# Keys, values and half of the queries of an attention stage as seven block products in two groups, in a one-core encoder trunk

## The chip, the core and the metric

The kernel runs on one core of a Trainium2 chip. The metric is the device time of one execution in microseconds (us). Engines are called as in the profile: PE is TensorE (matrix products), PEld its weight loads, DVE is VectorE, ACT is ScalarE, POOL is GpSimd, SP is SyncE, which issues most DMAs.

## What is computed

Two layers of an encoder run on 768 tokens of width 1024 (512 of one request and 256 of another). Each layer adds half a SwiGLU feed-forward block, a token mixer, and another half block, each on the RMS-normed stream. The first mixer is a gated recurrence (HGRN2); the second, the one that is changed, is windowed attention:

```python
def window_gqa_mixer(x, w_qkv, w_o, sinks):
    q, k, v = jnp.split(x @ w_qkv, [Hq * d, Hq * d + Hk * d], axis=-1)   # 1024 | 256 | 256 columns
    q = rope_partial(q.reshape(B, T, Hq, d))      # 16 heads of 64; the first 16 dims are rotated
    k = rope_partial(k.reshape(B, T, Hk, d))      # 4 heads
    ...
    s = jnp.einsum('bnqhgd,bnkhd->bnhgqk', qb, kband) * (d ** -0.5)   # blocks of 128, one to each side
    s = jnp.where(mask, s, -jnp.inf)
    m = jnp.maximum(jnp.max(s, axis=-1, keepdims=True), sink)
    p = jnp.exp(s - m)
    denom = jnp.sum(p, axis=-1, keepdims=True) + jnp.exp(sink - m)
    o = jnp.einsum('bnhgqk,bnkhd->bnqhgd', p / denom, vband)
    return o.reshape(B, T, Hq * d) @ w_o
```

Everything is float32. The products of weights and activations are made as three matmuls each, from a high and a low part of both factors: the high part is the value rounded to a format that TensorE takes at full rate, the low part is what is left. Making the two parts is a "split": a cast on ScalarE, then a subtraction on VectorE.

## The kernel before

The 768 tokens are six blocks of 128 rows; a half is three blocks. Python code writes out all instructions; a scheduler then gives each engine a fixed order, by the order of the code and by when it expects operands and buffers to be ready.

**Seven products.** Most large products of the kernel are made by a scheme of Strassen's kind: for a group, both factors are seen as 2x2 blocks, and seven block products p1 to p7 (instead of eight) with sums of blocks before and after give the result. FACTOR (line 58) names the activation factor of each product, a block b00, b10, b11 or a sum t1 to t4; `h_sums` (1374) makes the four sums and their splits. The weight factors are made in `quad_steps` (232): p1, p2, p3 and p4 use blocks as they are, p5's weight is summed by a DMA that adds in place (`into`, lines 163 and 164, issued by POOL), p7's by another, and p6's and p3's by an addition on VectorE (line 290). The order of the products is in ORDERS.

**Weights.** `load_next` (166) loads the next planned weights into raw buffers (four, tag wr; a quad needs all four); `stage_next` splits the next one into buffers of tag w (eight; a block product takes two). `ahead` stages as far as buffers allow whenever a product is done.

**The normed input.** As the last matmuls of the feed-forward block end, `norm_block` (396) norms each block of rows, and `turn` (454) transposes a half of it in two parts. For the row of this attention stage (row 4) it writes the high part from PSUM on ScalarE (485) and the low part on VectorE (486). For the HGRN stage (row 1) it first keeps the value (482) and then splits it (349, 350), since the sums t1 to t4 need it.

**The HGRN stage** makes its values by the seven products, in two groups over the inner dimension: `v_quad` (1377), matmuls in line 1399, results in lines 1410 to 1416, closing corrections in 1422 and 1423.

**The attention stage**, `swa` (1440): `proj_tok` (977) makes keys and values of all six blocks, 24 plain matmuls a block (the helper `mm3`, lines 344 to 346); `put_kv` rotates the keys (1428 to 1435), transposes and splits them (1459, 349, 350) and copies the values (1453). Then follow the queries, in two projections q0 and q1 of 512 columns, each cut into 24 pieces of six matmuls. Eight pieces run ahead; the other 40 are interleaved with the attention units. A unit (class Unit) is one block and one group of four heads; there are 24. It transposes its queries (1639), makes scores (1653), maxima (1669), exponentials (1682), sums and scaling (1688 to 1698), transposes the probabilities (1705, 1707), multiplies them with the values (1714), and splits the result. `pipeline` (1579) gives each unit four steps of a list in time: scores of unit i at step 4i, together with the values of unit i - 2; probabilities from step 4i + 5 on. `extra` puts the query pieces on steps -4 to 58, the reload of x on step 46, and pieces of the output projection from step 60 on. The stream x is spilled to memory by one deferred step (`spill_x`, 962) and reloaded later, so that its buffers can hold queries.

## Time and profile before

| | |
|---|---|
| median of 3 runs | 2718.07 us (2716.32 to 2718.52) |
| the profiled execution | 2717.88 us, span of its instructions 2716.1 us |
| mean granted TensorE clock | 0.999 |
| busy: PE, PEld, DVE, ACT, POOL | 100%, 91%, 80%, 50%, 9% |
| attention stage, first projection to first output piece | 1961.4 to 2120.2 us of the span |
| HGRN values, the 252 matmuls of line 1399 | 531.0 to 588.0 us of the span |

In profile lines, L12 is line 12 of the kernel; a group has the line, engine, operation, output and input tiles, shapes and count, then busy time, the mean duration of one in ns, and the idle time of the engine ahead of them with what ended it. Tiles: ps is PSUM, w are split weights, wr raw ones, big the arena of activations, x the stream's buffers, tA and tB temporaries. A stretch (a line that begins with two times) gives its length, then the busy time of PE, PEld, DVE, ACT and POOL with their instruction counts, the granted clock, the DMA share and GB/s. A line of the order of time gives start, duration, engine, source line, operation and count. Matmuls overlap: the time from start to start is what one costs.

### The profile page before, as it was taken

To read this page: it belongs to the slowest core of one execution; us is meant where nothing else is said; L and a number is where in the kernel's file an instruction comes from. 1 tells how busy PE (TensorE), PEld (TensorE's weight loads), DVE (VectorE), ACT (ScalarE), POOL (GpSimd) and SP (SyncE) were. 2 spreads that over 40 slices of the span, in tenths; PEclk is the share of its full clock that TensorE was granted. 3 is DMA by queue.
4 is the path that set the end of the run, shared out by engine and by line. 5 is a ranking of instruction groups with operands and counts; after the bars stand their busy time and mean duration, and the time that the engine had idled before them with its cause. 6 is when DMAs were issued, how large, how long until landed. Compare 5 with 4: busy or idle time off the path is not lost.

```text
span 2716.1 us, 44725 instructions
## 1 busy us (share of the span) xinstructions
PE 2703.0 (100%) x17197; PEld 2466.8 (91%) x17197; DVE 2181.3 (80%) x3914; ACT 1361.7 (50%) x2555; POOL 243.2 (9%) x285
## 2 busy tenths in 40 slices
PE   9999999999999999999999999999999999999998
PEld 9999999889888889999999999999987789999997
DVE  8888788887776779878888978787847769787887
ACT  6444444746666464444446444444546664444443
POOL 1111110000000011111111111110000011111010
PEclk9999999999999999999999999999999999999999
DMA  6554554441110446455444655544412136555443
GB/s 184 136 125 116 129 140 125 124 113 45 49 44 22 147 101 152 120 140 139 125 119 110 152 133 140 129 123 116 135 62 79 48 69 153 134 142 129 117 116 106
DMA packets 347446, 311.31 MB, mean 115 GB/s; under 512 B 12680, under 2 KB 268384, under 8 KB 347232
## 3 DMA queue, kind: packets, MB, share of 16 engines
q1 hardware_dynamic: 304336, 218.66, 26.9%
q0 software_dynamic: 38592, 76.30, 16.2%
q10 hardware_dynamic: 4304, 13.49, 1.4%
q8 instruction: 135, 2.21, 0.3%
q14 instruction: 79, 0.65, 0.1%
HBM read 222.68 MB, written 9.44 MB: 85 GB/s over the span
## 4 chain that ended last, share of the span: by engine, by line
PE 95%; DVE 3%; DMA 1%; ACT 1%; issue 1%; DVEq 0%; SPq 0%; ACTq 0%; POOLq 0%
PE ps L622 45%; PE ps L786 19%; PE ps L344 7%; PE ps L345 7%; PE ps L346 7%; PE ps L1399 2%; PE ps L1075 1%; PE ps L821 1%; PE ps L1714 1%; PE ps L1705 1%; PE ps L1223 1%; PE ps L1653 1%; DVE x L849 1%; PE ps L473 1%; DVE big L350 1%
## 5 line engine op out<-in xcount | busy, mean ns | idle before, releaser
L622 PE MATMUL ps<-big,w 128*128 128x384 f32 x7224 | 1262.9, 334 | 1.4 <-ACT tA L641 1.1
L622 PEld LDWEIGHTS ps<-big,w 128*128 128x128 f32 x7224 | 1252.9, 188 | 5.6 <-ACT tA L641 1.7
L262 ACT CAST w<-wr 128x512 fp32r<-128x512 f32 (+1 forms) x642 | 451.4, 714 | 734.0 <-DVE wr L290 310.7
L263 DVE TENSOR_TENSOR w<-wr,w 128x512 fp32r<-128x512 f32 (+1 forms) x642 | 511.9, 802 | 215.4 <-ACT w L262 150.8
L786 PE MATMUL ps<-w,big 128*128 128x512 f32 x2520 | 578.5, 390 | 0.7 <-DVE x L849 0.5
L786 PEld LDWEIGHTS ps<-w,big 128*128 128x128 f32 x2520 | 472.1, 188 | 100.6 <-DVE x L849 3.6
L849 DVE SCALAR_TENSOR_TENSOR x<-ps,x 128x512 f32<-128x512 f32 x468 | 303.1, 682 | 6.2 <-PE ps L346 6.2
L164 POOL DMA_DIRECT2D s<-wr x132 | 117.2, 930 | 1229.5 <-DMA wr<-in_ffn_w_dram 461.1
L349 ACT CAST big<-tA 128x384 fp32r<-128x384 f32 x296 | 148.2, 512 | 146.3 <-DVE tA L665 38.5
L164 POOL DMA_DIRECT2D wr<-wr x133 | 117.2, 900 | 1062.3 <-DVE tA L1317 337.5
L344 PE MATMUL ps<-w,big 128*128 128x512 f32 x480 | 194.5, 405 | 0.0
L346 PE MATMUL ps<-w,big 128*128 128x512 f32 x480 | 187.9, 391 | 0.0
L345 PE MATMUL ps<-w,big 128*128 128x512 f32 x480 | 187.6, 391 | 0.0
L350 DVE TENSOR_TENSOR big<-tA,big 128x384 fp32r<-128x384 f32 x296 | 160.5, 553 | 8.0 <-ACT big L349 7.7
L344 PE MATMUL ps<-big,w 128*128 128x512 f32 (+2 forms) x448 | 153.4, 344 | 0.4 <-issue 0.3
L345 PE MATMUL ps<-big,w 128*128 128x512 f32 (+2 forms) x448 | 151.0, 337 | 1.0 <-DVE big L350 0.7
L346 PE MATMUL ps<-big,w 128*128 128x512 f32 (+2 forms) x448 | 150.8, 337 | 0.0
L290 DVE TENSOR_TENSOR wr<-wr,wr 128x512 f32<-128x512 f32 (+1 forms) x126 | 110.6, 878 | 0.0
L344 PEld LDWEIGHTS ps<-w,big 128*128 128x128 f32 x480 | 90.3, 188 | 22.0 <-issue 4.6
L346 PEld LDWEIGHTS ps<-w,big 128*128 128x128 f32 x480 | 90.1, 188 | 19.8 <-issue 0.4
L263 DVE TENSOR_TENSOR w<-s,w 128x512 fp32r<-128x512 f32 x132 | 90.4, 686 | 20.3 <-ACT w L262 20.3
L211 DVE TENSOR_TENSOR w<-wr,w 128x1024 fp32r<-128x1024 f32 (+1 forms) x68 | 81.7, 1206 | 30.2 <-ACT w L208 22.7
(227 smaller groups left out, 2964.3 us busy)
## 6 DMA issues: line engine op xcount, KB each, us to landing
wr<-in_ffn_w_dram SPq DMA_DIRECT2D x270, 512.0 KB, 3.8
s<-wr POOLq DMA_DIRECT2D x132, 256.0 KB, 5.0
s<-in_ffn_w_dram SPq DMA_DIRECT2D x126, 256.0 KB, 3.4
wr<-wr POOLq DMA_DIRECT2D x110, 256.0 KB, 4.3
wr<-in_hg_w_in_dram SPq DMA_DIRECT2D x40, 512.0 KB, 3.8
wr<-wr POOLq DMA_DIRECT2D x23, 512.0 KB, 6.0
spill<-x ACTq DMA_DIRECT2D x12, 512.0 KB, 3.1
x<-spill ACTq DMA_DIRECT2D x12, 512.0 KB, 3.2
```

The lines of the kernel that those rows point to most:

```text
L164: self.nc.gpsimd.dma_start(out, src, accum_op=ALU.add)
L262: nc.scalar.copy(h, src)
L263: low = nc.vector.tensor_sub(l, src, h.bitcast(F32)).ins
L290: nc.vector.tensor_add(into, into, term)
L344: nc.tensor.matmul(out, a[0], b[0], start=first, stop=False)
L345: nc.tensor.matmul(out, a[0], b[1], start=False, stop=False)
L346: nc.tensor.matmul(out, a[1], b[0], start=False, stop=last)
L349: self.cast = self.nc.scalar.copy(hi, src).ins
L350: return self.nc.vector.tensor_sub(lo, src, hi.bitcast(F32)).ins
L622: self.nc.tensor.matmul(ps, a[x], b[y], start=first and k == 0 and i == 0, stop=k == 3 and i == 2, skip_group_check=True,)
L786: nc.tensor.matmul(ps, a[x], w[y], start=name == chain and kp == 0 and q == 0, stop=kp == 1 and q == 2, skip_group_check=True,)
L849: return self.nc.vector.scalar_tensor_tensor(x, ps, c, x, ALU.mult, ALU.add).ins
```

## The change

The two projections "kv" and "q0" are replaced by two groups of seven block products, as in `v_quad`, whose inner part becomes `tok_product`. The columns are keys and values as block column 0, the first query half as block column 1. p1 and p2 of both groups, which need the first half of the rows alone, come first, from four weight loads of their own ("front"); the remaining five products of each group follow in the order "rest", from quads that load their four weight blocks again. Results go to six buffers of x, so x is spilled block by block as it is normed. `turn` now writes every mixer's input as it did for row 1. Keys of the first three blocks are rotated, transposed and split among the products of the first group; the first three blocks of queries after p6 of the second; the rest after the last product. Of q1's 24 pieces four run ahead of the units, and 20 are put on steps -4 to 45.4, 2.6 steps apart. The places of the output pieces stay.

```diff
+ORDERS["rest"] = ORDERS["down"][2:]
...
-            if len(srcs) < 4:
+            if len(srcs) < 4 and how != "front":
                 src = src.rearrange("(k p) c -> p k c", p=P)
...
-            hi, lo = (t[:, half * H : (half + 1) * H] for t in self.h[m])
-            nc.scalar.activation(hi, pt, AF.Copy, scale=g)
-            nc.vector.scalar_tensor_tensor(lo, pt, g, hi.bitcast(F32), ALU.mult, ALU.subtract)
-        for k in range(2 if row == 1 else 0):
+            nc.scalar.activation(self.block(m % 2, half, m // 2), pt, AF.Copy, scale=g)
+        for k in range(0 if feeds_ffn else 2):
             self.split(self.tn[(k, half)][:, part], *(t[:, :, half * H : (half + 1) * H] for t in self.hl[(k, part)]))
...
         self.norm_block(b)
+        if row == 4:
+            self.spill_x(range(b, b + 1))
...
     def plan_swa(self, w_qkv, w_o):
-        for tag, c in (("kv", D), ("q0", 0), ("q1", 512)):
-            self.plan_tok(tag, w_qkv, c)
+        parts = [self.quarters(w_qkv[n * 512 : (n + 1) * 512, :], (D, 0)) for n in range(2)]
+        for n in range(2):
+            for name, src in zip(("p1", "p2"), parts[n]):
+                self.queue.append((("kvq", n, name), (src,), (2, 512), "front"))
+        for n in range(2):
+            self.plan_quad(("kvq", n), parts[n], (2, 512), "rest")
+        self.plan_tok("q1", w_qkv, 512)
         self.plan_out("sw_o", w_o)
...
+    def rotate_here(self, t, heads, pos):
+        nc = self.nc
+        x = t.rearrange("p (h d) -> p h d", d=HD)
+        c, sn = (self.rope[:, pos, i, :].unsqueeze(1) for i in range(2))
+        h2 = RD // 2
+        rv = self.tmp(heads * RD).rearrange("p (h d) -> p h d", d=RD)
+        nc.vector.tensor_mul(rv[:, :, :h2], x[:, :, h2:RD], sn[:, :, :h2].to_broadcast([P, heads, h2]))
+        nc.vector.tensor_mul(rv[:, :, h2:], x[:, :, :h2], sn[:, :, h2:].to_broadcast([P, heads, h2]))
+        nc.vector.tensor_mul(x[:, :, :RD], x[:, :, :RD], c.to_broadcast([P, heads, RD]))
+        nc.vector.tensor_add(x[:, :, :RD], x[:, :, :RD], rv)
...
     def swa(self, next_row):
-        self.later(self.spill_x)
+        qtok, own = {}, [self.xt() for _ in range(HB)]
...
+        for n in range(2):
+            for name in ("p1", "p2"):
+                self.tok_product("kvq", n, name, cols)
+                self.run_later()
+            if n == 0:
+                self.h_sums(0)
+        self.run_later(len(self.deferred))
         kT = [[self.big([P, 2, T], F32R) for _ in range(2)] for _ in range(KV // 2)]
         vv = self.big([P, NBLK, KV, HD])
...
-        self.drain(self.proj_tok("kv", put_kv))
...
+        for n in range(2):
+            for name in ORDERS["rest"]:
+                self.tok_product("kvq", n, name, cols)
+                if n == 0 and name == "p7":
+                    self.h_sums(1)
+                if n == 0 and name in ("p5", "p4", "p6"):
+                    keys(("p5", "p4", "p6").index(name))
+                if n and name == "p6":
+                    for i in range(HB):
+                        x21 = cols(i, 1)
+                        nc.vector.tensor_add(x21, x21, cols(HB + i, 1))
+                        queries(i)
+        for i in range(HB):
+            x12 = cols(HB + i, 0)
+            nc.vector.tensor_sub(x12, x12, cols(HB + i, 1))
+            keys(HB + i)
+        for i in range(HB):
+            queries(HB + i)
...
-        q = itertools.chain(self.proj_tok("q0", put_q(0)), self.proj_tok("q1", put_q(1)))
+        q = self.proj_tok("q1", put_q)
         wo = self.out_proj("sw_o", 0, act, None)
-        for _ in range(8):
+        for _ in range(4):
             next(q)
         piece = lambda g: lambda: next(g, None)
-        extra = [(i * 9 / 8 - 4, piece(q)) for i in range(16)]
-        extra += [(14 + i * 44 / 23, piece(q)) for i in range(24)]
+        extra = [(i * 2.6 - 4, piece(q)) for i in range(20)]
         extra.append((46, self.reload_x))
         extra += [(60 + i * 3 / 2, piece(wo)) for i in range(22)]
```

In `tok_product`, which holds the former inner loop of `v_quad`, the results of the first group are copied by ScalarE for p1, p2, p4 and p3, and all others are added or subtracted by VectorE out of PSUM, as before in `v_quad`.

More of the change, by code (lines that the diff above doesn't have):

```diff
@@ L544 @@
     xn = [None] * NBLK
+    banks = {}
     normed = mixed = first = halved = None
@@ L584, in plan_ffn, with quarters @@
             self.plan((tag, "last", c), w2[(NF - 2) * P :, c * 512 : (c + 1) * 512], (2, 512))
+    @staticmethod
+    def quarters(w, starts=(0, 512)):
+        rows = w.rearrange("(a k p) c -> k p a c", p=P, k=2)
+        return [rows[k][:, :, c : c + 512] for c in starts for k in range(2)]
     def plan_down(self, key, w, order="down"):
-        rows = w.rearrange("(a k p) c -> k p a c", p=P, k=2)
-        srcs = [rows[k][:, :, c * 512 : (c + 1) * 512] for c in range(2) for k in range(2)]
-        self.plan_quad(key, srcs, (2, 512), order)
+        self.plan_quad(key, self.quarters(w), (2, 512), order)
     def up_plain(self, tag, j, half):
@@ L960, in ffn, with spill_x @@
                 self.run_later()
-    def spill_x(self):
-        self.spill = self.dp.tile([NBLK, P, D], F32, name=self.name("spill"))
-        for b in range(NBLK):
+    def spill_x(self, blocks=range(NBLK)):
+        if not blocks[0]:
+            self.spill = self.dp.tile([NBLK, P, D], F32, name=self.name("spill"))
+        for b in blocks:
             self.nc.scalar.dma_start(self.spill[b], self.x[b])
-        self.x = [None] * NBLK
+            self.x[b] = None
     def reload_x(self):
@@ new lines, in tok_product @@
+        wh, wl = self.take((tag, n, name))
+        chain = {"p2": "p1", "p4": "p5", "p3": "p7"}.get(name, name)
+        for i in range(HB):
+            if name == chain:
+                self.banks[(chain, i)] = self.ps()
+            ps = self.banks[(chain, i)]
+            sl = slice(i * P, (i + 1) * P)
+            for k in range(2):
+                a, w = factor(FACTOR[name], k, sl), (wh[:, k, :], wl[:, k, :])
+                for q, (x, y) in enumerate(((0, 0), (0, 1), (1, 0))):
+                    nc.tensor.matmul(
+                        ps,
+                        a[x],
+                        w[y],
+                        start=name == chain and k == 0 and q == 0,
+                        stop=k == 1 and q == 2,
+                        skip_group_check=True,
+                    )
+            x22 = cols(HB + i, 1)
+            x = {"p2": cols(i, 0), "p4": cols(i, 1), "p3": cols(HB + i, 0)}.get(name, x22)
+            if n == 0 and name == "p1":
+                nc.scalar.mul(x, ps, -1.0)
+            elif n == 0 and x is not x22:
+                nc.scalar.copy(x, ps)
+            elif name in ("p1", "p5"):
+                nc.vector.tensor_sub(x, x, ps)
+            else:
+                nc.vector.tensor_add(x, ps, x)
@@ L1418, in v_quad @@
+        self.done((tag, n, name))
+    def v_quad(self, n, dst):
+        cols = lambda b, c: dst[b][:, c * 512 : (c + 1) * 512]
+        for name in ORDERS["down"]:
+            self.tok_product("v", n, name, cols)
             if n == 0 and name == "p7":
@@ L1442, in swa, with cols, keys @@
         self.load_bands()
-        self.later(self.spill_x)
+        qtok, own = {}, [self.xt() for _ in range(HB)]
+        def cols(b, c):
+            if b < HB and c == 0 or b >= HB and c == 1:
+                return own[b % HB][:, c * 512 : (c + 1) * 512]
+            while len(own) < NBLK:
+                own.append(self.xt())
+            return own[HB + b % HB][:, c * 512 : (c + 1) * 512]
+        def keys(gb):
+            src = cols(gb, 0)
+            pos = gb if gb < TA // P else gb - TA // P
+            st = self.tmp(512).rearrange("p (g a d) -> p g a d", a=2, d=HD)
+            self.rotate(src[:, :256], KV, pos, st[:, :, 0, :])
+            nc.gpsimd.tensor_copy(st[:, :, 1, :], st[:, :, 0, :])
+            nc.scalar.copy(vv[:, gb], src[:, 256:].rearrange("p (g d) -> p g d", d=HD))
+            pt = self.ps()
+            for g in range(KV):
+                col = st[:, g].rearrange("p a d -> p (a d)")
+                nc.tensor.transpose(pt[:, g * P : (g + 1) * P], col, self.ident)
+            for i in range(KV // 2):
+                src = pt[:, i * 2 * P : (i + 1) * 2 * P].rearrange("p (g t) -> p g t", g=2)
+                self.split(src, *(t[:, :, gb * P : (gb + 1) * P] for t in kT[i]))
@@ new lines, in queries @@
+        def queries(gb):
+            t = cols(gb, 1)
+            s, pos = (0, gb) if gb < TA // P else (1, gb - TA // P)
+            self.rotate_here(t, 512 // HD, pos)
+            for gg in range(2):
+                qtok[(s, pos, gg)] = t[:, gg * 256 : (gg + 1) * 256]
+        for n in range(2):
[5 more added lines that the diff above has]
+        self.run_later(len(self.deferred))
@@ L1482, in swa @@
+        hold = []
         of = {}
```

87 lines of the change are left out of this document (15 added, 72 removed).

## The prediction

> **What bounds the kernel now.** I read the page first, then the stretches around the attention stage, then the instructions in order of time on TensorE and VectorE.
>
> ```profile
> span 2716.1 us, 44725 instructions
> PE 2703.0 (100%) x17197; PEld 2466.8 (91%) x17197; DVE 2181.3 (80%) x3914; ACT 1361.7 (50%) x2555; POOL 243.2 (9%) x285
> PE 95%; DVE 3%; DMA 1%; ACT 1%; issue 1%; DVEq 0%; SPq 0%; ACTq 0%; POOLq 0%
> ```
>
> TensorE is busy in 2703.0 of 2716.1 us and is 95% of the chain that ended last. Time can come only from fewer or cheaper matmuls, and it is kept only if nothing makes TensorE wait afterwards. The stretches say how much room the other engines have:
>
> ```profile
> core 0: us, PE busy (x) PEld busy (x) DVE busy (x) ACT busy (x) POOL busy (x), PEclk, DMA share, GB/s
> 1900.00:1920.00 20.00, 20.00 (x99) 17.70 (x98) 19.65 (x32) 7.88 (x14) 2.61 (x3) 1.00 0.69 176
> 530.90:545.00 14.10, 14.10 (x64) 11.68 (x63) 14.10 (x19) 11.02 (x17) 0.17 (x1) 1.00 0.36 113
> 1961.40:2023.10 61.70, 61.70 (x306) 51.00 (x305) 29.36 (x86) 25.36 (x58) 2.40 (x6) 1.00 0.26 90
> 2023.10:2086.00 62.90, 62.90 (x425) 48.05 (x423) 44.95 (x175) 42.52 (x125) 0.00 (x0) 1.00 0.23 76
> 2086.00:2120.20 34.20, 34.20 (x242) 25.20 (x240) 24.68 (x100) 25.43 (x79) 0.00 (x0) 1.00 0.14 47
> ```
>
> The last three are the stage that is changed, from the first matmul of the key and value projection (1961.4) to the first piece of the output projection (2120.2), 158.8 us. TensorE never pauses; VectorE is busy 99.0 us (29.36 + 44.95 + 24.68), and least of all at the head, 48%. The first two lines are the fullest VectorE that I found: 98% and 100% for 14 to 20 us, with TensorE unbroken beside it.
>
> **Fewer matmuls.** Keys, values and the first query half are now 2 projections x 6 blocks x 8 x 3 = 288 matmuls of 512 columns. They become 2 groups x 7 products x 18 = 252. The same products run in the HGRN stage for the values:
>
> ```profile
> L1399 PE MATMUL ps<-w,big 128*128 128x512 f32 x252 | 57.3, 389 | 0.0
> ```
>
> 57.3 / 252 = 0.2274 us each, so 36 fewer are 8.2 us. Second, 40 pieces of six matmuls stand between units today and 20 will (24 of the second query half, 4 of them ahead of the units).
>
> ```profile
> 2098.40 0.38 PE L1639 MATMUL ps<-ident_r,big 128*128 128x128 f32 x2
> ...
> 2102.92 0.48 PE L344 MATMUL ps<-w,big 128*128 128x512 f32 x1
> ...
> 2104.39 0.38 PE L1639 MATMUL ps<-ident_r,big 128*128 128x128 f32 x2
> 2110.72 0.38 PE L1639 MATMUL ps<-ident_r,big 128*128 128x128 f32 x2
> 2118.02 0.38 PE L1639 MATMUL ps<-ident_r,big 128*128 128x128 f32 x2
> ```
>
> A piece started at 2102.92 and the next work at 2104.39: 1.47 us for six matmuls that take 1.36 in a stream. The switch costs 0.11, and 20 fewer are 2.1 us. Together TensorE has **10.3 us** less to do. Transposes are as many as before.
>
> **What VectorE gets for it.** It issues in this rhythm in the HGRN value stage:
>
> ```profile
> 540.06 0.95 DVE L516 TENSOR_TENSOR big<-big,big 128x768 f32<-128x768 f32 x1
> 540.93 0.68 DVE L1414 TENSOR_TENSOR x<-x,ps 128x512 f32<-128x512 f32 x1
> 541.52 1.22 DVE L263 TENSOR_TENSOR w<-wr,w 128x1024 fp32r<-128x1024 f32 x1
> 542.66 0.68 DVE L1414 TENSOR_TENSOR x<-x,ps 128x512 f32<-128x512 f32 x1
> 543.26 1.22 DVE L290 TENSOR_TENSOR wr<-wr,wr 128x1024 f32<-128x1024 f32 x1
> 544.39 0.68 DVE L1414 TENSOR_TENSOR x<-x,ps 128x512 f32<-128x512 f32 x1
> 544.99 0.95 DVE L350 TENSOR_TENSOR big<-big,big 128x768 fp32r<-128x768 f32 x1
> 545.86 1.22 DVE L263 TENSOR_TENSOR w<-wr,w 128x1024 fp32r<-128x1024 f32 x1
> L486 DVE SCALAR_TENSOR_TENSOR big<-ps,cols,big 128x384 fp32r<-128x384 f32 x16 | 8.8, 610 | 3.5 <-ACT big L485 3.5
> ```
>
> From start to start: 0.6 us for a result added out of PSUM, 1.14 for a weight split or a sum of two weight blocks, 0.87 for a sum or split of 768 activations. Added:
> - results: 14 products x 3 row blocks, 12 of them copied by ScalarE, so 30 x 0.6 = 18.0; six closing corrections, 3.6
> - sums of the normed input: 2 groups x (4 sums + 4 splits) x 0.87 = 13.9
> - weights: 14 splits and 4 sums where 8 splits were, 10 x 1.14 = 11.4
> - the input's own low parts, 8 x 0.87 for the 8.8 us of line 486: 1.8 less.
>
> That is **45.1 us** more: 144.1 us of VectorE work in a stretch of 158.8 - 10.3 = 148.5 us, 97%. So the whole stage fits, barely; the question is where within it.
>
> At the head TensorE has 57.3 us of products, and transposes (24 of the input's second half, 12 of keys):
>
> ```profile
> L473 PE MATMUL ps<-ident_r,big 128*128 128x128 f32 x264 | 35.3, 273 | 0.0
> 1987.53 0.23 DVE L1431 TENSOR_TENSOR tA<-ps,big 128x64 f32<-128x64 f32 x1 [4.16 <-ACT tA L1428]
> 1987.68 0.18 DVE L1433 TENSOR_TENSOR tB<-ps,big 128x32 f32<-128x32 f32 x1
> 1987.77 0.18 DVE L1434 TENSOR_TENSOR tB<-ps,big 128x32 f32<-128x32 f32 x1
> 1988.02 0.42 DVE L350 TENSOR_TENSOR big<-ps,big 128x256 fp32r<-128x256 f32 x1
> 1988.37 0.22 DVE L1435 TENSOR_TENSOR tA<-tA,tB 128x64 f32<-128x64 f32 x1
> ```
>
> 36 x 0.134 = 4.8, so 62.1 us. VectorE has there, norms left out, 18.0 for results, 1.8 for three corrections, 13.9 for sums, 22.8 for twenty weight steps (two early splits, ten of the quads, four sums, four splits of the second query half), 5.2 for six input splits, 5.0 for three blocks of keys (the five lines add up to 1.65 with the split counted twice) and, estimated at 1 us each from the same four rotation lines on twice the width, 3.0 for three blocks of queries: 69.7 us, **7.6 too many**. Behind it come three corrections, three blocks of keys and three of queries, 9.8 us, beside four pieces (5.9) and the key transposes (1.6), 7.5: 2.3 more. So at the first unit's scores VectorE is 9.9 us behind if it never idles, and the units' maxima queue behind those keys and queries on VectorE, for which TensorE then waits. The lower end: the closing 9.8 us is not needed by units 0 and 1 (they see keys 0 to 2), so 0.1 if all of it slips behind them. I take 4, nearer to the lower end, because the nearest row, the value stage, shows TensorE unbroken beside a full VectorE.
>
> Edits that I cost at nothing: spilling x block by block (0.33 us of ScalarE's queue each, under the last matmuls of the FFN), and ScalarE's 12 copies, since it is busy 41% of the head (25.36 of 61.7). The quads lose p1 and p2 as cover ahead of p5, whose weight is summed by a DMA that adds in place:
>
> ```profile
> 540.17 22.16 SPq L175 DMA_DIRECT2D wr<-in_hg_w_in_dram  x4
> 544.83 0.87 POOL L164 DMA_DIRECT2D wr<-wr  x1 [32.07 <-DVE wr L290]
> DMA to landing us min/median/max: 4.3/5.0/6.4
> ```
>
> In the value stage the second group's load starts at 540.17, the adding DMA issues at 544.83 and lands by 552.1 at the latest; cast and split (1.05 and 1.22) make p5's weight ready at 554.4. The first group's last product ends 7 x 18 x 0.2274 after 530.9, at 559.6: 5 us of cover without p1 and p2. If the load had to wait for p3's split (5 us later) the cover would be gone, at about 1 us a group.
>
> **Units with fewer pieces.** From the starts above a unit is 5.99 to 7.30 us with two pieces, so 3.05, 3.4 or 4.4 of its own, by its key blocks and those of its neighbours. The others need per unit:
>
> ```profile
> L1669 DVE CUSTOM_DVE_ANT_0 big<-ps,big,nsinks 128x256 f32<-128x256 f32 (+1 forms) x96 | 45.9, 522 | 3.7 <-PE ps L1653 3.7
> L1698 DVE TENSOR_SCALAR big<-big,stat 128x256 f32<-128x256 f32 (+1 forms) x96 | 29.5, 370 | 0.5
> L350 DVE TENSOR_TENSOR tA<-ps,tA 128x256 fp32r<-128x256 f32 x24 | 10.0, 416 | 0.9 <-ACT tA L349 0.8
> L1682 ACT ACTIVATE big<-big,stat 128x256 f32<-128x256 f32 (+1 forms) x96 | 51.1, 535 | 0.9 <-DVE stat L1669 0.9
> L1707 ACT COPY tA<-ps 128x512 f32<-128x512 f32 x56 | 30.8, 580 | 12.9 <-PE ps L1705 12.9
> ```
>
> With a second split like the third line, VectorE needs (45.9 + 29.5 + 20.0) / 24 = 4.0 us, ScalarE (51.1 + 30.8 and two casts like those splits) 4.2, with the small steps on stat some 4.4. With 20 pieces over 12.4 units TensorE has about 3.4 + 2.4 = 5.8, still the longest; where only one piece falls, 4.5, which is level. I put 1 us there, between 0 and 4.8 (five units with one piece, short by up to 0.95: a piece of 1.47 less about 0.5 of slack ahead of the transposes). From step 45.4, the last piece, to step 60, the first of the output projection, there is **none**: units 12 to 14 give TensorE 3.05 + 3.4 + 3.7 = 10.1 us (estimates from those starts), the others 12.5 to 13.2. I take 2.7; at the low end, output pieces that move forward, 0.
>
> **The sum.** -10.3 + 4 + 1 + 2.7 = -2.6. The profiled execution took 2717.88 us (span 2716.1 and 1.8 around it), against a median of 2718.07, so the two may be used alike: **2715.3**. All costs at their low ends: -10.3 + 0.1 = -10.2; at their high ends: -10.3 + 9.9 + 4.8 + 3.2 = +7.6. 0.2%, about what can be told from no change here, is 5.4 us.
>
> **Rivals.** *The cover holds*, as in the value stage: the order of instructions lets the closing work of the head slip among units, and pieces are drawn into the holes. For it: VectorE full and TensorE unbroken in the two rows above. Against: those lasted 20 us, not 62. It costs 0 to 3 us: 2707.6 to 2710.6, say 2709. Chance 0.36.
>
> *VectorE becomes the bound of the head and the queue carries it into the units* (slower). Results wait in PSUM behind sums and weight splits, products wait for banks, and the first unit's maxima wait behind the last keys. It decides once VectorE idles even 5 us while the first sums wait for ScalarE (the input's casts come ahead of them): then all 9.9 and these 5 are on the path, with the units' and the gap's 4.8 and 3.2. -10.3 + 22.9 gives 2730.5, and 2726.5 with units and gap at half; from 2723 on I count it here. Against: VectorE's total still fits. Chance 0.16.
>
> *TensorE's clock.* In every row above the granted clock is 1.00, and no pause in this stage tests it. If one pause let it fall to half while two products of 8.2 us run, they cost 8.2 more: 2723.5. For it: only a head whose waits come in one piece. Chance 0.03. [...]
>
> *It doesn't do what it says*: the 36 matmuls are gone by count, so only a stage that isn't on the path could hide them, and TensorE is the path. Not given a chance.
>
> **How the numbers follow.** The sum above holds 0.45, with a range of its own of 2711 to 2722; about 0.02 of it lies under -5.4. Faster by over 0.2%: 0.36 + 0.02 = 0.38. Slower: 0.16 + 0.03 = 0.19. Within: 0.43. The range runs from the full saving, 2707, into the slower rival, 2726, and leaves out some 2 in 10 of the chance, most of it above.
>
> **What would show it.** The head: 252 matmuls of the product's line in about 57.3 us if unbroken; every us above that is waiting, and its releasers should be VectorE's results, sums and weight splits. VectorE should be over 90% busy there. Between the last query piece and the first output piece, TensorE's idle time should be near 2.7 us with softmax steps as releasers. The forecast is wrong if TensorE shows no idle time at all there (then the cover holds), or if it idles more than 12 us in the stage, or if the waits are for the adding DMAs.

## The result and the profile after

The changed kernel takes **2751.99 us** (median of 4 runs, 2751.41 to 2752.96) against 2718.24 us (2716.32 to 2718.52 in 4 runs) before: a ratio of 1.0126, 95% interval 1.0109 to 1.0144. It is 33.8 us **slower**; the forecast was 2.6 us faster, and its range ended at 2726. The profiled span grew from 2716.1 to 2750.6 us, so 34.5 us are to be found in the trace.

First the page of the changed kernel: the span, the busy times, and the group of the block products (504 matmuls: 252 of the HGRN values as before, 252 new).

```profile
span 2750.6 us, 44790 instructions
PE 2710.7 (99%) x17161; PEld 2468.1 (90%) x17161; DVE 2228.3 (81%) x3970; ACT 1382.1 (50%) x2585; POOL 250.1 (9%) x291
L1400 PE MATMUL ps<-w,big 128*128 128x512 f32 x504 | 121.8, 403 | 6.8 <-DVE x L1415 5.4
```

TensorE has 36 instructions fewer (17161 for 17197), as the change says. Yet it is busy 7.7 us longer, and idle for 39.9 us of the span (2750.6 - 2710.7), where it was 13.1. VectorE grew by 47.0 us; I had counted 45.1. So the work is what was forecast. What TensorE waited for is in the view of its waits (line waited at, releaser, us in total, times, longest):

```profile
PE ps L1479 <- POOL tA L1474: 13.2, 3, 6.7
PE ps L1751 <- DVE big L1744: 5.9, 5, 2.0
PE ps L1400 <- DVE x L1415: 5.4, 2, 5.3
PE ps L1400 <- ACT x L1411: 1.1, 1, 1.1
```

L1479 is the transpose of a block of keys, waiting for a copy on GpSimd; L1751 is a unit's transpose of probabilities, waiting for their scaling; L1400 are the block products, waiting for results. Before, TensorE had no wait longer than 1.1 us in the whole trace. Now the stage in three stretches, cut at the first score of unit 0 and at those of units 15 and 23. The changed kernel:

```profile
core 0: us, PE busy (x) PEld busy (x) DVE busy (x) ACT busy (x) POOL busy (x), PEclk, DMA share, GB/s
1961.90:2064.80 102.90, 82.06 (x342) 65.06 (x342) 81.82 (x152) 50.34 (x89) 8.31 (x11) 0.88 0.38 109
2064.80:2154.30 89.50, 82.11 (x571) 58.14 (x570) 66.32 (x268) 63.26 (x196) 0.00 (x0) 0.98 0.18 60
2154.30:2214.70 60.40, 60.40 (x401) 45.51 (x400) 43.83 (x158) 39.16 (x121) 0.00 (x0) 1.00 0.07 19
```

The kernel before, cut at the same three scores:

```profile
1961.40:2016.70 55.30, 55.30 (x272) 45.67 (x270) 25.20 (x66) 21.17 (x47) 2.40 (x6) 1.00 0.29 100
2016.70:2118.30 101.60, 101.60 (x679) 77.31 (x678) 72.58 (x289) 70.25 (x207) 0.00 (x0) 1.00 0.18 58
2118.30:2178.50 60.20, 60.20 (x401) 45.25 (x400) 45.26 (x160) 38.73 (x118) 0.00 (x0) 1.00 0.14 44
```

The head went from 55.3 to 102.9 us, units 0 to 15 from 101.6 to 89.5, and from unit 15 on nothing changed. The head had to grow, since 18 query pieces that stood behind unit 0's first score now stand ahead of it, and the units had to shrink by as much. How much that is was measured in a kernel that moves these pieces and changes nothing else (e4, below): its head takes 79.8 us, 24.5 more, which is 18 pieces of six matmuls at 0.2274. That gives the account:

- **The head:** 79.8 - 8.2 (36 matmuls) is 71.6. It took 102.9: **31.3 us lost**.
- **The units up to the 23rd:** 101.6 + 60.2 - 24.5 is 137.3. They took 149.9: **12.6 us lost**.
- Together -8.2 + 31.3 + 12.6 = 35.7, beside the 34.5 of the spans; the stage starts 0.5 us later and 1.7 us come back behind unit 23, which I didn't follow.

Three places in the head show what happens there. TensorE, in order of time:

```profile
1984.70 4.47 PE L1400 MATMUL ps<-w,big 128*128 128x512 f32 x19
1994.44 5.46 PE L1400 MATMUL ps<-w,big 128*128 128x512 f32 x12 [5.27 <-DVE x L1415]
...
2021.21 1.12 PE L1479 MATMUL ps<-ident_r,tA 128*128 128x128 f32 x4 [5.65 <-POOL tA L1474]
2021.97 23.12 PE L1400 MATMUL ps<-w,big 128*128 128x512 f32 x90
2051.81 1.54 PE L1479 MATMUL ps<-ident_r,tA 128*128 128x128 f32 x6 [6.72 <-POOL tA L1474]
```

At 1989.17 a product has to wait 5.27 us for one result (L1415) to leave PSUM. VectorE in that time:

```profile
1988.07 2.69 DVE L351 TENSOR_TENSOR big<-big,big 128x768 fp32r<-128x768 f32 x3
1990.68 1.88 DVE L1417 TENSOR_TENSOR x<-ps,x 128x512 f32<-128x512 f32 x3
1992.48 1.22 DVE L291 TENSOR_TENSOR wr<-wr,wr 128x1024 f32<-128x1024 f32 x1
1993.61 1.28 DVE L1415 TENSOR_TENSOR x<-x,ps 128x512 f32<-128x512 f32 x2
```

It never stops; the result that TensorE needs stands fourth, behind splits, other results and a weight sum. At 2015.56 TensorE comes to the transposes of the third block of keys, 5.65 us before they are ready, with products behind them in its queue. At 2045.09 it comes to those of the last three blocks, 6.72 us before they are ready, and behind them stand the first pieces of q1, which could have run, as e1 shows.

### The profile page after: what moved, and what is told of

Read it like the earlier page. It is cut to its first block, busy times and chain, and to the rows that moved or that the text cites. A ratio compares the mean times of both kernels' runs of the same rounds, so it can differ in the third digit from the quotient of the medians.

```text
span 2750.6 us, 44790 instructions
## 1 busy us (share of the span) xinstructions
PE 2710.7 (99%) x17161; PEld 2468.1 (90%) x17161; DVE 2228.3 (81%) x3970; ACT 1382.1 (50%) x2585; POOL 250.1 (9%) x291
## 4 chain that ended last, share of the span: by engine, by line
PE 94%; DVE 4%; ACT 1%; issue 0%; DMA 0%; POOL 0%; ACTq 0%; DVEq 0%; POOLq 0%
PE ps L620 46%; PE ps L784 19%; PE ps L345 6%; PE ps L346 6%; PE ps L347 6%; PE ps L1400 3%; PE ps L1074 1%; PE ps L819 1%; PE ps L1751 1%; PE ps L1222 1%; PE ps L1760 1%; PE ps L1699 1%; DVE big L351 1%; PE ps L470 1%; DVE x L847 0%
## 5 line engine op out<-in xcount | busy, mean ns | idle before, releaser
L263 ACT CAST w<-wr 128x512 fp32r<-128x512 f32 (+1 forms) x650 | 459.8, 718 | 746.2 <-DVE wr L291 317.3
L264 DVE TENSOR_TENSOR w<-wr,w 128x512 fp32r<-128x512 f32 (+1 forms) x650 | 522.2, 808 | 217.4 <-ACT w L263 153.4
L784 PEld LDWEIGHTS ps<-w,big 128*128 128x128 f32 x2520 | 472.2, 188 | 100.5 <-DVE x L847 3.7
L1400 PE MATMUL ps<-w,big 128*128 128x512 f32 x504 | 121.8, 403 | 6.8 <-DVE x L1415 5.4
L1400 PEld LDWEIGHTS ps<-w,big 128*128 128x128 f32 x504 | 97.4, 195 | 28.4 <-issue 5.7
L291 DVE TENSOR_TENSOR wr<-wr,wr 128x1024 f32<-128x1024 f32 (+1 forms) x130 | 115.6, 889 | 0.0
L209 ACT CAST w<-wr 128x1024 fp32r<-128x1024 f32 (+1 forms) x66 | 67.8, 1029 | 72.6 <-PE ps L346 28.2
```

The lines of the kernel that those rows point to most:

```text
L263: nc.scalar.copy(h, src)
L264: low = nc.vector.tensor_sub(l, src, h.bitcast(F32)).ins
L784: nc.tensor.matmul(ps, a[x], w[y], start=name == chain and kp == 0 and q == 0, stop=kp == 1 and q == 2, skip_group_check=True,)
L1400: nc.tensor.matmul(ps, a[x], w[y], start=name == chain and k == 0 and q == 0, stop=k == 1 and q == 2, skip_group_check=True,)
```

## The experiments

Times are medians; the kernel before took 2717.5 to 2718.4 us beside them. "Head" is from the first product of the stage, which starts between 1961.1 and 1963.3 us of these spans, to the first score of unit 0.

| kernel | us | ratio to before, 95% interval | head, us |
|---|---|---|---|
| e1_keys_late | 2740.42 | 1.0082 (1.0053 to 1.0112) | 89.6 |
| e2_copy_act | 2753.35 | 1.0130 (1.0101 to 1.0159) | 102.8 |
| e3_fill | 2753.81 | 1.0132 (1.0102 to 1.0161) | 100.0 |
| e4_few_pieces | 2731.29 | 1.0051 (1.0032 to 1.0071) | 79.8 |
| e5_pool_low | 2749.13 | 1.0117 (1.0087 to 1.0146) | 99.1 |
| e6_deep | 2722.06 | 1.0018 (1.0007 to 1.0030) | 79.8 |
| e7_spread | 2726.44 | 1.0029 (1.0016 to 1.0043) | 74.4 |
| e8_all | 2742.04 | 1.0091 (1.0061 to 1.0120) | 98.9 |
| e9_no_low | 2738.41 | 1.0075 (1.0046 to 1.0104) | 85.5 |
| e10_cast_pool | 2744.71 | 1.0098 (1.0069 to 1.0128) | 92.5 |
| e11_late_deep | 2731.52 | 1.0051 (1.0028 to 1.0074) | 88.0 |
| e12_no_low_second | 2727.56 | 1.0035 (1.0023 to 1.0047) | 83.4 |
| e13_pool_low_second | 2730.94 | 1.0045 (1.0025 to 1.0064) | 87.5 |
| e14_sums_early | 2730.10 | 1.0042 (1.0022 to 1.0062) | 89.2 |
| e15_sums_pool | 2731.56 | 1.0047 (1.0028 to 1.0067) | 87.7 |
| e16_copies_twice | 2733.43 | 1.0057 (1.0035 to 1.0080) | 91.7 |

### The order on TensorE: e1_keys_late

The transposes and splits of the key blocks are put into a list and issued behind the first four pieces of q1. (All six blocks' are, though later expectations speak of the last three. Of the two long waits one is at the third block and one at the last three.)

```diff
         nc.scalar.copy(vv[:, gb], src[:, 256:].rearrange("p (g d) -> p g d", d=HD))
-        pt = self.ps()
+        def turn():
+            pt = self.ps()
...
+        turns.append(turn)
...
         for _ in range(4):
             next(q)
+        for turn in turns:
+            turn()
```

> The changed kernel, but the transposes and splits of all six blocks of keys are issued behind the four first pieces of the second query half; their rotation and copies stay where they are. Theory 1 (order on TensorE: the transposes stand in TensorE's fixed order ahead of products and pieces that are ready, and wait there for a chain through VectorE and GpSimd): most of the 13.2 us of waits before the key transposes goes, and the slow clock behind two of them: 2730 to 2740 us instead of 2752. Theory 2 (VectorE's total is the bound of the head): the same wait comes back at results, weight splits or the first units, 2747 us or more.

11.6 us of the 33.8 are gone, 13.3 of the head:

```profile
1961.40:2051.00 89.60, 79.72 (x340) 63.51 (x340) 79.23 (x149) 49.73 (x87) 7.36 (x11) 0.92 0.45 125
```

The same instructions take 89.6 us in place of 102.9 in another order: the transposes come later on TensorE, and with them the splits of the keys on ScalarE and VectorE. So the order was part of the cause; 18.0 us over the 71.6 stay.

### GpSimd's copy and the clock: e2_copy_act, e3_fill

TensorE's longest waits name the copy on GpSimd. e2 makes it on ScalarE:

```diff
-            nc.gpsimd.tensor_copy(st[:, :, 1, :], st[:, :, 0, :])
+            nc.scalar.copy(st[:, :, 1, :], st[:, :, 0, :])
```

> The changed kernel, but the copy of the rotated keys, which GpSimd made, is made by ScalarE. Theory 3 (GpSimd's queue: the copy stands behind the DMAs that add weights in place, which wait for loads): the 13.2 us of waits that the profile puts down to GpSimd go, 2735 to 2742 us. Theories 1 and 2: the copy begins within 0.25 us of the end of the rotation that it reads, so GpSimd is only the last link: 2752 within 3 us.

No gain: the releaser named last was only the last link of a chain that came late on VectorE. e3 puts matmuls into the three longest pauses, on operands that are there anyway and into a bank that nobody reads, so that TensorE's clock doesn't fall (behind each of the three it is 0.50 in the changed kernel, last section):

```diff
+        def fill(n):
+            idle = self.ps()
+            for _ in range(n):
+                nc.tensor.matmul(idle, self.identr, self.hl[(0, 0)][0][:, 0, :512], start=True, stop=True)
...
+                if n == 0 and name == "p5":
+                    fill(20)
...
+            if gb in (2, 3):
+                fill(24)
```

> The changed kernel with 68 matmuls of 512 columns that nobody reads, 20 of them behind p5 of the first group and 24 each ahead of the key transposes of blocks 2 and 3, where TensorE paused 5.3, 5.7 and 6.7 us; 15.5 us of work at full clock, and nothing waits less. Theory 4 (the pauses let the clock fall to half, and the products behind them run slow): the granted clock stays at 1.00 through the head and the time falls by 4 to 12 us, to 2740 to 2748. If the slow products come from something else (memory, PSUM shared with VectorE), the clock row and the time stay, or the time rises by the part of the 15.5 us that doesn't fit: 2752 to 2760.

```profile
1962.20:2062.20 100.00, 92.10 (x410) 72.99 (x410) 81.56 (x152) 50.58 (x89) 8.44 (x11) 0.98 0.39 112
```

The granted clock of the head rises from 0.88 to 0.98, and the head becomes only 2.9 us shorter, the whole run not at all. Less the 15.5 us of the fill, TensorE is busy for 76.6 us in place of 82.1, so the clock was worth 5.5 us of its work. But fill and idle time together take 23.4 us where the idle time took 20.8: what TensorE gains it waits for again. How much of that the fill itself causes isn't shown.

### Fewer pieces between units: e4_few_pieces, e6_deep, e7_spread

e4 is the kernel *before*, with its own plain products. Only the pieces move: 28 ahead of the units in place of 8, and 20 between them, 2.6 steps apart as in the change.

```diff
-        for _ in range(8):
+        for _ in range(28):
             next(q)
...
-        extra = [(i * 9 / 8 - 4, piece(q)) for i in range(16)]
-        extra += [(14 + i * 44 / 23, piece(q)) for i in range(24)]
+        extra = [(i * 2.6 - 4, piece(q)) for i in range(20)]
```

> The kernel before, with its plain projections of keys, values and the first query half, but with 28 query pieces ahead of the units and 20 between them, at the steps of the changed kernel. TensorE has the same matmuls, and 20 fewer switches (2 us). Theory 5 (with this few pieces the units themselves make TensorE wait, whatever the head): 2722 to 2732 us, idle time at the transposes of probabilities. Theory 6 (the units of the changed kernel lost their 14 us to what VectorE carried over from the head and to the slow clock): 2714 to 2720 us.

13.6 us slower than the kernel before beside it (2717.7), with the same work. Its stretches, cut at the same scores (its first product starts at 1962.63):

```profile
1962.30:2042.40 80.10, 80.10 (x382) 66.31 (x380) 34.60 (x92) 27.91 (x56) 2.41 (x6) 1.00 0.30 96
2042.40:2131.80 89.40, 80.86 (x571) 57.33 (x570) 66.63 (x271) 63.19 (x195) 0.00 (x0) 0.98 0.19 60
2131.80:2192.20 60.40, 60.21 (x401) 45.15 (x400) 43.20 (x154) 39.24 (x121) 0.00 (x0) 1.00 0.06 19
```

Its waits on TensorE begin with this one:

```profile
PE ps L1704 <- DVE big L1697: 6.4, 6, 2.4
```

The head is unbroken and the units lose it all, 89.4 us as in the changed kernel. Yet VectorE is busy only 66.6 and ScalarE 63.2 of these 89.4 us: no engine is full. TensorE waits for the scaling (L1697) that ends a unit's chain of scores, maxima, exponentials and sums. e6 leaves everything as in e4, but turns the probabilities four steps later and takes the values one unit later:

```diff
-        for i in range(len(units) + 2):
+        for i in range(len(units) + 3):
...
-            done = units[i - 2] if i > 1 else None
+            done = units[i - 3] if i > 2 else None
...
-                at(t + 5 + j, 1, lambda u=u, j=j: u.probs(j))
+                at(t + 9 + j, 1, lambda u=u, j=j: u.probs(j))
```

> The kernel before with 28 pieces of the second query half ahead of the units and 20 between them (2731.3 us), and the units' chain one step longer: a unit's probabilities are turned and its values taken one unit later than now. If units with fewer pieces lose time because a unit's chain from scores through maxima, exponentials and normalisation takes longer than the two units of other work that cover it, the cover grows by one unit and units 0 to 15 take 76 to 83 us in place of 89.4: 2718 to 2725. If they lose it because VectorE or ScalarE have too much to do per unit, no change: 2730 to 2733. If it is the buffers that the softmax tiles share, slower than 2733.

```profile
2041.00:2119.40 78.40, 77.19 (x552) 55.53 (x551) 63.69 (x259) 60.05 (x189) 0.00 (x0) 1.00 0.21 68
2119.40:2179.80 60.40, 60.24 (x399) 45.83 (x398) 45.70 (x166) 40.40 (x125) 0.00 (x0) 1.00 0.06 19
```

9.2 of the 13.6 us come back with the same amount of work, and units 0 to 15 take 78.4 us. It is the length of a unit's chain that decides, not what an engine has to do. Of the 4.4 that stay, 1.5 lie ahead of unit 23 (138.8 in place of 137.3) and some 3 behind it, where one unit more is still to be finished. e7 goes the other way: e4 with 24 pieces ahead (`range(24)`) and 24 between, on to step 55.8.

> The kernel before with 24 pieces of the second query half ahead of the units and 24 between them, one each 2.6 steps as in the kernel with 28 and 20, but on to step 56 in place of 45, so that no stretch without pieces is left ahead of the output projection. If the loss of 13.6 us with 28 and 20 lies mostly in the stretch without pieces, 2720 to 2723. If each piece taken from between the units costs the same, about 0.68 us (13.6 for 20), 16 of them cost 10.9: 2728 to 2729.

4.9 us less than e4 for four pieces, 1.2 us each, where the 20 cost 0.68 each on average. So the stretch without pieces ahead of the output projection was the dearest, but neither theory has the size: it is about a third of the loss.

### The rest of the head: e5, e8, e9, e10, e11

With the keys late, the head takes 89.6 us for work that needs 71.6, and VectorE is busy 79.2 of them. Three ways were tried to unload it or its suppliers; all stand on e1. e5 subtracts the quads' low parts on GpSimd:

```diff
-                low = nc.vector.tensor_sub(l, src, h.bitcast(F32)).ins
+                eng = nc.gpsimd if key[0] == "kvq" else nc.vector
+                low = eng.tensor_sub(l, src, h.bitcast(F32)).ins
```

> The changed kernel with the transposes of keys 3 to 5 behind the first four pieces of q1 (as in the kernel that took 2740.4 us), and with the low parts of the second to fifth weights of both groups (ten of the fourteen products) subtracted on GpSimd: some 14 to 20 subtractions of 1.1 us leave VectorE, at about 2.6 us each on GpSimd. If VectorE's total work is what still bounds the head (78.7 of 89.1 us busy there, with its results late), the head becomes 6 to 12 us shorter: 2729 to 2734. If the head waits for ScalarE's casts and copies (17.97 of its first 18.1 us busy) or for the order in which results come, the same 2740 within 2 us. If GpSimd is too slow for the weights, products wait for them instead: over 2743.

e9 leaves them out and multiplies the high part in their place. The main product of these weights is then added twice, so this is no longer the same computation, and its time alone is read:

```diff
-                low = nc.vector.tensor_sub(l, src, h.bitcast(F32)).ins
+                if key[0] == "kvq":
+                    low = cast.ins
+                else:
+                    low = nc.vector.tensor_sub(l, src, h.bitcast(F32)).ins
+            if key[0] == "kvq":
+                lo = hi
```

> The changed kernel with late key transposes (2740.4 us), and without the low parts of the ten quad weights of the head: the high part is multiplied in their place, so TensorE has the same matmuls and the result is less exact. Some 12 us of subtractions leave VectorE (78.7 of 89.1 us busy in that head) and nothing is put in their place. If VectorE's amount of work is what bounds the rest of the head, nearly all of the 12 comes off: 2728 to 2732. If ScalarE bounds it (17.97 of the first 18.1 us busy there, and VectorE's idle time behind it), little does: 2737 to 2741.

e10 casts the quads' weights on GpSimd:

```diff
-                nc.scalar.copy(h, src)
+                (nc.gpsimd.tensor_copy if key[0] == "kvq" else nc.scalar.copy)(h, src)
```

> The changed kernel with late key transposes, and with the ten quad weights of the head cast on GpSimd in place of ScalarE: 10.5 us leave ScalarE, some three casts of them in the first 18 us. If ScalarE at the start of the head is what holds the rest up, VectorE gets its input earlier and the head becomes 3 to 6 us shorter: 2734 to 2737. If VectorE's amount is the bound, 2739 to 2741. If casts on GpSimd take so long that products wait for weights, over 2742.

By their times, e5 and e10 (2749 and 2745 us) would have GpSimd too slow for the weights, and e9 (2738) would have ScalarE as the bound. The traces give other reasons: TensorE's longest wait in the head is for a norm in e5 and e9 (6.7 and 6.3 us), and for a cast of activations in e10 (6.2 us). e5, in order of time:

```profile
1969.47 1.77 POOL L165 DMA_DIRECT2D s<-wr  x2 [19.43 <-DMA wr<-in_sw_w_qkv_dram]
...
1976.77 1.23 DVE L292 TENSOR_TENSOR wr<-wr,wr 128x1024 f32<-128x1024 f32 x1 [6.17 <-issue]
```

With the low parts off VectorE, the scheduler put a weight sum (L292) ahead of the last norm in VectorE's queue. The sum writes a raw block that the two DMAs read, to add it to p7's weight, so it has to wait until they have landed; it starts 7.3 us after their issue. VectorE stands still for 6.17 us, at a place where TensorE had nothing else: the transposes behind that norm waited 6.7 us. e9 has the same pause, 5.85 us. So these two don't tell what VectorE's amount is worth. Besides, e5 took little off VectorE: with 12 subtractions fewer (one of 1024 columns takes GpSimd 2.34 us) it is busy for 80.2 us of the head, where e1 has 79.2. In e10 VectorE's own instructions became longer (last section), and its busy time in the head rose from 79.2 to 84.0 us with no instruction added. e8 is e5 with the longer chain of e6:

> The changed kernel with all three: late key transposes, low parts of the quads' weights on GpSimd, and the units' chain one step longer. If head and units lose time independently, their gains add up: 2740.4 less 0 to 11 for GpSimd and less 6 to 13 for the chain, 2716 to 2734. If one of the two edits does nothing by itself it does nothing here either.

It is 7.1 us faster than e5, so the chain counts here too, and e5's edit stays a loss. e11 is e1 with the longer chain alone:

> The changed kernel with late key transposes and the units' chain one step longer. If the loss in the units stands by itself, the edit is worth here what it was worth without the new head, 9.2 us: 2730 to 2732. If the units of the changed kernel wait behind VectorE's work left over from the head, it is worth less: 2734 to 2740.

2731.5, 8.9 us less than e1, where e6 gained 9.2 on e4: the loss in the units and the loss in the head stand side by side. Its head is read in all and in three slices:

```profile
1963.20:2051.20 88.00, 77.31 (x342) 61.60 (x342) 79.14 (x149) 49.45 (x87) 7.36 (x11) 0.96 0.45 127
1963.20:1981.20 18.00, 15.80 (x76) 12.32 (x77) 12.82 (x17) 17.87 (x32) 1.77 (x2) 1.00 0.54 153
...
2001.20:2011.20 10.00, 6.98 (x31) 5.45 (x29) 6.33 (x9) 3.66 (x6) 2.14 (x3) 1.00 0.92 219
2011.20:2051.20 40.00, 35.60 (x156) 29.05 (x156) 39.99 (x94) 16.11 (x31) 2.18 (x4) 0.91 0.38 115
```

VectorE is busy 79.1 us, 7.5 more than the 71.6 that TensorE needs, and idle for 8.9: 5.2 in the first 18 us, where ScalarE is full, and 3.7 in the ten from 2001.2. In the last 40 us it never stops. What it waits for in the whole head:

```profile
DVE w L264 <- ACT w L263: 4.8, 2, 3.7
DVE big L351 <- ACT big L350: 2.1, 2, 1.4
DVE stat L405 <- ACT stat L404: 0.8, 1, 0.8
DVE w L212 <- ACT w L209: 0.7, 1, 0.7
```

All four are for ScalarE, 8.4 of the 8.9 us: casts of weights and of the input, and a norm. But the longest, 3.7 us, doesn't come from a full ScalarE, which is busy only 3.66 of these ten us. In order of time:

```profile
1999.34 0.87 POOL L165 DMA_DIRECT2D wr<-wr  x1 [27.15 <-DVE wr L291]
...
2005.66 2.00 ACT L263 CAST w<-wr 128x1024 fp32r<-128x1024 f32 x2 [4.94 <-DMA wr<-wr]
2006.74 2.36 DVE L264 TENSOR_TENSOR w<-wr,w 128x1024 fp32r<-128x1024 f32 x2 [3.67 <-ACT w L263]
```

The DMA that adds in place, for p5's weight of the second group, is issued at 1999.34, and ScalarE's cast of that weight starts 6.3 us later. ScalarE waits 4.94 us for it, VectorE 3.67 us for ScalarE, and the sums that stand behind these splits on VectorE come late: TensorE waits 4.4 us for the cast of one of them. The changed kernel has the same waits at this place, 3.43 us on ScalarE and 3.32 on VectorE. No run issues this DMA earlier, so what it costs the run isn't measured.

### Amount or order on VectorE: e12 to e15, and ScalarE: e16

All five stand on e11. e12 is e9's edit for the second group alone (`key == ("kvq", 1)`), where e9's pause ahead of the norm doesn't come back. It, too, adds a product twice in place of the low part, and only its time is read.

> The changed kernel with late key transposes and the units' chain one step longer (2731.5 us), without the low parts of the second group's five quad weights (the high part is multiplied in their place, the result is less exact). 6 us of subtractions leave VectorE, and the order of its queue ahead of them stays. If VectorE's amount of work bounds the second half of the head (19.99 of 20 and 11.00 of 11 us busy there), 2725 to 2728. If the head is bounded by what happens before, the late sums of the second half with their 4.4 us wait, and the order, 2730 to 2732.

```profile
1962.50:2045.80 83.30, 75.01 (x340) 58.98 (x340) 73.49 (x143) 49.22 (x87) 8.22 (x11) 1.00 0.47 135
```

VectorE has 5.6 us less to do and the head is 4.6 us shorter, the run 4.0 in the medians (4.7 against the kernel before beside each). The order isn't quite the same, though: the sums of the second half of the input start at 2002.21, where e11 has 2009.02, since no split that waits stands ahead of them. e14 leaves the amount and moves only these sums ahead:

```diff
-                if n == 0 and name == "p7":
+                if n == 0 and name == "p5":
                     self.h_sums(1)
```

> The changed kernel with late key transposes and the longer chain (2731.5 us), with the input sums of the second group issued behind p5 of the first group in place of p7, so ahead of the first keys on VectorE. The amount of work is the same. If order is the cause, the wait of 4.4 us for the sums' cast goes, and the slow matmuls behind it: 2725 to 2728. If VectorE's amount is the bound, the wait comes back later, at a result or a bank: 2730 to 2732.

2730.1 (2728.5 to 2732.7), no clear difference from e11: the 4.4 us wait for the sums' cast is gone, and a wait of 2.65 us for a weight's cast and slower matmuls stand in its place. (That weight is again p5's of the second group; its cast had waited 3.80 us for the adding DMA.) So the amount of VectorE's work counts in this head, and the place of these sums by itself doesn't. e13 and e15 let GpSimd make the second group's low parts, without and with the early sums:

> As the one without the second group's low parts, but GpSimd computes them, at about 2.6 us each: nothing is left out. If GpSimd's results come in time, the same time within 1 us. If VectorE's weight sum or the products wait for GpSimd, over 2731.

> Early sums and the second group's low parts on GpSimd together. If both amount and order cost time, the gains add: 2720 to 2725. If the two are the same wait seen twice, no better than the better of the two, 2725 to 2728.

Both within 0.6 us of e11. In e13's head VectorE has lost the same subtractions as in e12, but is busy 78.2 us, 0.9 less than in e11 and not 5.6:

```profile
1962.80:2050.30 87.50, 78.89 (x341) 62.12 (x341) 78.25 (x143) 49.44 (x87) 21.79 (x17) 0.94 0.46 128
```

What left VectorE made the rest of its work slower (last section). e16 makes ScalarE's twelve copies of results twice:

```diff
+            again = 2 if tag == "kvq" else 1
             if n == 0 and name == "p1":
-                nc.scalar.mul(x, ps, -1.0)
+                for _ in range(again):
+                    nc.scalar.mul(x, ps, -1.0)
```

(and the same for `nc.scalar.copy`, which makes the copies of p2, p4 and p3).

> The changed kernel with late key transposes and the longer chain (2731.5 us), with ScalarE's twelve copies of the first group's results from PSUM made twice: 6.5 us more on ScalarE, half of it in the first 20 us, none on VectorE. If ScalarE at the start is on the path (it is busy 17.97 of the first 18.1 us, and VectorE idles 5.2 us behind it), the head becomes 3 to 6 us longer: 2734 to 2738. If VectorE's amount of work alone decides, the same within 1 us.

The run is 1.9 us longer and the head 3.7, from a start that came 2.0 us earlier in this profile, for some 6.5 us of work. So ScalarE is partly on the path: the run moves less than the one theory had and more than the other. What VectorE's idle time would be with less work on ScalarE wasn't settled: e10, which took casts away from it, changed VectorE's speed as well.

No kernel here beats the one before. The best that computes everything and has the new products is e14 with 2730.1, 11.7 us slower, and not clearly apart from e11, e13 and e15.

## Why the prediction was wrong

**Fewer matmuls, right in count.** 36 instructions are gone from TensorE. No run shows the 8.2 us by themselves, though the price of 0.2274 came out again in the 18 moved pieces. The 2.1 us of switches can't be told from the units' loss, which is larger.

**VectorE's excess in the head, the step that failed first.** The ledger itself held: 69.7 + 9.8 = 79.5 us of VectorE work, and 79.1 to 81.8 were measured in the heads of the changed kernel, e1 and e11, with the norms that the ledger leaves out. The end of the range was 9.9. What failed is "I take 4, nearer to the lower end, because the nearest row, the value stage, shows TensorE unbroken beside a full VectorE". That row lasted 14 us, over which results may wait in PSUM without stopping TensorE (argued, not tested); here the backlog builds up for 88 us, and e12 gives back 4.6 us for 5.6 us of work. With the keys late the head (e11's) loses 16.4 us, not 4: 7.5 for the amount and 8.9 for VectorE's idle time, which the sum put at nothing ("if it never idles") and only a rival priced, at 5.

**The order of the key transposes, not in the prediction.** I set the last keys and queries "beside four pieces (5.9) and the key transposes (1.6)", as if the pieces would run meanwhile. In TensorE's queue the transposes stand first, so the pieces wait with them, 6.72 us. The transposes of the first three blocks stand ahead of products in the same way, and TensorE waits 6.5 us there. e1 moves all of them to a later place, which is worth 13.3 us of the head and 11.6 of the run, a term that no case of the prediction had; the share of the closing ones alone wasn't measured. It could have been seen in the code: `keys` ends in transposes, and products or the four pieces come after it.

**Units with fewer pieces.** I took 1 + 2.7 us, with 4.8 + 3.2 as the high ends; it is 13.6 (e4). I compared what each engine has to do per unit: VectorE 4.0 and ScalarE 4.4 against TensorE's 5.8, and found slack. But a unit's work goes back and forth between the engines, and its chain has to fit under the other work of two units. e6 lengthens that cover and returns 9.2 us without touching any engine's amount. The trace of before could not show the chain as a wait, because 40 pieces hid it.

**ScalarE's copies at nothing, "since it is busy 41% of the head".** An average: in the first 18 us of e11's head it is busy 17.87, and twelve copies more cost the run 1.9 us (e16).

**The adding DMAs, costed at nothing.** In the changed kernel no wait of TensorE is put down to a quad weight. But the 5 us of cover, read from the value stage, were not there for ScalarE and VectorE: the second group's DMA made ScalarE wait 3.43 us and VectorE 3.32 (4.94 and 3.67 in e11), and in e14 TensorE itself waited 2.65 us for the weight. The profile names a weight sum of VectorE (L291) as what released the DMA, so VectorE's lateness comes back by this way. In e5 and e9 the DMAs for p7's weight stopped VectorE's queue.

**The rivals.** "VectorE becomes the bound of the head and the queue carries it into the units" was the right mechanism for the head: its condition, VectorE idle for 5 us while the first sums wait for ScalarE, is met with 5.2, and its 14.9 us for the head stand beside 16.4, though it had no adding DMA in them. At 2730.5 it lacked the order of the key transposes (11.6) and 5.6 of the 13.6 us lost in the units, for which it had 8.0 by another mechanism. "TensorE's clock" happened as well, and it did fall to half, 0.50. But no run shows 8.2 us for it: in e3, which holds it up, TensorE's work takes 5.5 us less, the head is 2.9 us shorter, and the run not at all. "The cover holds" did not come.

**What would show it:** of the three signs named for a wrong forecast one came plainly, TensorE idle for more than 12 us in the stage (28 us in its first two stretches); waits for the adding DMAs came on ScalarE and VectorE. The releasers were named in part: in the head 5.4 us of TensorE's waits are for VectorE's results, and 13.2 for the keys. VectorE is 80% busy there (81.82 of 102.9), not over 90%: it waits at the beginning, and in the middle behind the DMA. Between the last query piece and the first output piece TensorE idles 4.7 us where 2.7 were forecast, for scalings and a split.

## What to carry to other kernels

Pieces of independent work between dependent steps are cover for a chain: before they are taken away, weigh the chain's length, not the engines' busy time, and lengthen the pipeline first. When a stage's second engine gets more to do than the first, take the excess as cost in full, with the time that it idles at the start; a short stretch that got by shows nothing of a long one. Read the code in each engine's own order: in these runs an instruction that waited held up what stood behind it, ready or not (in the changed kernel the first pieces of q1, 6.72 us). When a profile names an engine as what was waited for, ask what that engine waited for.

## What the runs showed of the hardware

**The clock after a pause.** Behind the pause of 5.27 us, 12 matmuls of 512 columns took 5.46 us, 0.455 each and double the 0.2274 of a stream, at a granted clock of 0.50. A stretch of these 12, and one soon after:

```profile
1994.50:1999.80 5.30, 5.30 (x12) 3.71 (x12) 5.30 (x13) 1.85 (x3) 1.66 (x2) 0.50 0.46 115
2003.10:2008.10 5.00, 5.00 (x24) 4.17 (x23) 2.45 (x5) 3.34 (x7) 1.19 (x2) 1.00 0.94 227
```

The pauses of 5.65 and 6.72 us went the same way: the granted clock is 0.50 from 2021.2 to 2026.2 and from 2051.8 to 2057.8. In e14 shorter pauses close together slowed it as well: behind 2.65 us, two matmuls and another 0.52 us, 21 matmuls took 7.94 us, 0.378 from start to start, and the granted clock of the 20 us from 2000.0 is 0.83. How long a pause has to be isn't measured.

**VectorE beside GpSimd.** In e10, VectorE in order of time, and then GpSimd:

```profile
2001.17 0.22 DVE L1437 TENSOR_TENSOR tA<-x,big 128x64 f32<-128x64 f32 x1
2001.30 1.81 DVE L1441 TENSOR_TENSOR tA<-tA,tB 128x64 f32<-128x64 f32 x1
...
2003.84 0.21 DVE L1441 TENSOR_TENSOR tA<-tA,tB 128x64 f32<-128x64 f32 x1
...
2009.83 2.38 DVE L504 TENSOR_TENSOR big<-big,big 128x768 f32<-128x768 f32 x1
...
2015.75 0.94 DVE L507 TENSOR_TENSOR big<-big,big 128x768 f32<-128x768 f32 x1
```

```profile
2001.64 1.38 POOL L263 CAST w<-wr 128x1024 fp32r<-128x1024 f32 x1
...
2009.68 1.70 POOL L263 CAST w<-wr 128x1024 fp32r<-128x1024 f32 x1
```

The same addition takes 0.21 us alone and 1.81 beside a cast on GpSimd, and a sum of 768 columns 2.38 for 0.94: VectorE loses 1.60 and 1.44 us, where the two casts take 1.38 and 1.70. The cause isn't shown. The sums above go the same way: VectorE is 4.8 us busier in e10 than in e1, and 4.8 us busier in e13 than in e12. In e13's head its four weight sums take 1.65 us each, in e11's 1.22.
